# Attention outputs split as they come, a second bias buffer, the second norm inside its operands' loop, and small products ordered behind columns

## The chip, the cores and the metric

The kernel runs on one core of one Trainium2 chip. The metric is the device time of one execution in microseconds (us); three executions of the kernel before took 1672.16, 1673.4 and 1676.07 us. The core has TensorE (PE, matrix products into PSUM), VectorE (DVE), ScalarE (ACT), GpSimd (POOL) and SyncE (SP, which here mostly issues DMAs).

## The reference

Two requests of 512 tokens, 1024 wide, go through the same two layers: layer 0 is a bidirectional RWKV-7 time mixing, layer 1 a neighbourhood attention over an 8 x 64 grid of tokens. Each layer has a norm before it and one after it.

```python
def _trunk(x, pre_norm_g, post_norm_g, rwkv_params, na_params):
    for i in range(DEPTH):
        xn = _rms_norm(x, pre_norm_g[i])
        h = _rwkv7_branch(xn, ...) if i % N_MIXERS == 0 else _natten_branch(xn, ...)
        x = x + _rms_norm(h, post_norm_g[i])
    return x

def _natten_branch(xn, w_in, b_in, rpb, w_o, b_o):
    proj = xn @ w_in + b_in
    q, k, v, z = jnp.split(proj, 4, axis=-1)
    o = _neighbourhood_attention(heads(q) * (HEAD_DIM ** -0.5), heads(k), heads(v), rpb)
    return (o.reshape(bsz, t, D_INNER) * jax.nn.silu(z)) @ w_o + b_o
```

In `_neighbourhood_attention` each token attends to its 8 x 16 window with a learned bias per head, through a softmax.

## The kernel before, in words

Activations lie with channels on the 128 partitions and the 512 tokens along the free axis: a (1024 x 512) activation is eight tiles of 128 x 512. The requests are s = 0 and s = 1.

A weight product is made in *columns*: one column is 128 output channels, 8 steps over k, and 3 matmuls a step, because every float32 operand is split into a high part (a cast on ACT, L377) and a low part (a subtraction on DVE, L378), and hi·hi, hi·lo and lo·hi are summed (L428 to L430, one PSUM bank `pg`, two banks in all). A column is 24 matmuls. Its weights come by two DMAs into three `raw` buffers and are split the same way into `whi` and `wlo`.

The program has two parts. Up to some 1170 us the recurrent scan of layer 0 runs, in an order planned by hand. Then `rest` runs, and there the order is made by the tile scheduler: instructions are recorded by generators that `run` interleaves in given shares, and the scheduler places each one by its priority (the order of recording, moved by `high_priority`) when its inputs are ready in its own timeline. What it fixes is the order of the instructions on each engine; each engine then works its list in that order. `behind` adds an ordering edge between two instructions of one engine, without a wait.

The steps of `rest`, in the order of recording:

- `inproj(0, ...)`: the last two groups of columns q, k, v, z of request 0; `qkvz` takes a column out of `pg` by a product with the norm's `rstd` on DVE (L1398) and stores it to DRAM.
- `heads(s, p)`: attention for a pair of heads, in two half-heads of two column blocks. Loads of bias, q, k, v; scores on PE (`sc`, L1442, one buffer); on DVE score plus bias with its maximum (L1453); exponent on ACT (L1456); reciprocal and scaling on DVE (L1457, L1458); transposes on PE (`pt`, L1460); copies on ACT (`pts`, L1463); the product with v on PE (`po`, L1475; v is transposed by L1429). Last, `po` is multiplied by the gate z on DVE (L1484). For s = 0 the result is kept as float32 (`oa`) and split later.
- `out0(1)`: the output columns of layer 0 for request 1 into the tiles `h`, with their sum of squares (L1315, L1325, L1327).
- `out1(0)`: the output columns of attention for request 0. It first splits all eight `oa` (`operands`), into the `act` buffers, then makes the columns (L1499 takes them out of `pg`), then `rstd`, then two last operations a tile on DVE (L1506, L1507) and the store of the result.
- `norm0(1)`: post-norm, residual and next norm's sum for request 1: `rstds`, then for each of 8 tiles two operations on DVE (L1358, L1359), a square on ACT (L1360) and a sum on DVE (L1364); all of it at a raised priority, through `ahead`. Then `x1n(1)` splits the eight tiles for the next product (L1379 on ACT, L1380 on DVE), into `act` buffers that `out1(0)` must have left.
- `by_token`: 32 transposes of `h` (L1518) in eight groups of four into `pm` banks, copied by ACT (L1520) and stored, for the last product.
- `inproj(1, ...)` with `heads(1, p)`, and `last()`.

`rstds` (L449) turns a sum of squares into 1/sqrt on every partition: four matmuls against ones (L456), a root on ACT (L459), a reciprocal and four diagonal tiles on DVE (L461, L464), four matmuls that spread them (L468), a copy on ACT (L470).

Of the kernel before, what the change touches and what calls it, by code (L numbers as in the profile page):

```python
# [11 lines left out]
F32 = mybir.dt.float32  # L12
F32R = mybir.dt.float32r
AF = mybir.ActivationFunctionType
ALU = mybir.AluOpType
# [4 lines left out]
P = 128  # L20
T = 512
D = 1024
KT = D // P
NP = 8
# [207 lines left out]
class Trunk:  # L232
# [6 lines left out]
    LA = -40  # L239
    LATER = (0, 40, 0, 0)  # L240
    POST4 = 0.2
    LAST = ("pg", "pg", "po", "pm")
# [6 lines left out]
    NA = 1000  # L249
    SUMS, SG, ZY = 0, 0, 2  # L250
    CH, FIRST, WFIRST = 100, 17, 3
    NVS = 2
# [169 lines left out]
    def gemm(self, w, x, tag):  # L422

        nc = self.nc
        ps = self.p(tag)
        for k in range(KT):
            hi, lo = w[k]
            nc.tensor.matmul(ps, hi, x[k][0], start=(k == 0), stop=False)  # L428
            nc.tensor.matmul(ps, hi, x[k][1], start=False, stop=False)  # L429
            nc.tensor.matmul(ps, lo, x[k][0], start=False, stop=(k == KT - 1))  # L430
            if k < KT - 1:
                yield
        return ps
# [12 lines left out]
        run(self.rstds(acc))  # L446
        return acc

    def rstds(self, acc):  # L449

        nc = self.nc
        free, room = self.bank()
        yield "P", free, room
        ps = self.p("pm", (P, 4))
        for c in range(4):
            nc.tensor.matmul(ps[:, c:c + 1], acc[:, c * P:(c + 1) * P], self.ones[:, 0:1], start=True, stop=True)  # L456
        yield "A"
        r = self.t("rs", (P, 4), 2)
        nc.scalar.activation(r, ps, AF.Sqrt, bias=self.eps[:, 0:1], scale=1.0 / D)  # L459
        yield "D"  # L460
        nc.vector.reciprocal(r, r)  # L461
        dg = self.tmp()
        for c in range(4):
            nc.vector.tensor_scalar(dg[:, c * P:(c + 1) * P], self.ident, r[:, c:c + 1], None, op0=ALU.mult)  # L464
        yield "P", free, lambda c: max(room(c), c.at([dg.tensor.name]))
        out = self.p("pm")
        for c in range(4):
            nc.tensor.matmul(out[:, c * P:(c + 1) * P], self.ones, dg[:, c * P:(c + 1) * P], start=True, stop=True)  # L468
        yield "A"
        nc.scalar.copy(acc, out)  # L470

# [867 lines left out]
    def norm0(self, s):  # L1339

        nc = self.nc
        if s == 0:
            yield "P", lambda: ("h", s) in self.made
            self.x1_acc = self.t("vs", bufs=self.NVS)
            yield from self.rstds(self.h_acc)
            self.made.add(("hr", s))
            yield "P", lambda: self.did["x1s"] == KT, lambda c: c.at([self.x1_acc.tensor.name])
            yield from self.rstds(self.x1_acc)
            self.x1_rstd = self.x1_acc
            self.made.add(("x1", s))  # L1350
            return
        rstd = self.h_acc
        yield from self.rstds(rstd)
        acc = self.t("vs", bufs=self.NVS)
        for k in range(KT):
            h = self.h[k]
            x = self.load(self.t("xr", bufs=self.NXR), self.a["xc"][s][k * P:(k + 1) * P, :])
            nc.vector.scalar_tensor_tensor(h, h, self.vec("post0", k), rstd, op0=ALU.mult, op1=ALU.mult)  # L1358
            nc.vector.tensor_tensor(h, h, x, op=ALU.add)  # L1359
            nc.scalar.activation(x, h, AF.Square)  # L1360
            if k == 0:
                nc.scalar.activation(acc, h, AF.Square)
            else:
                self.adder(s, k + 1).tensor_tensor(acc, x, acc, op=ALU.add)  # L1364
            yield
        yield "P"
        yield from self.rstds(acc)
        self.x1_rstd = acc
        self.made.add(("x1", s))

    def adder(self, s, k):
        return self.nc.vector if s and k % 2 else self.nc.vector

    def x1n(self, s):

        out = []
        for k, h in enumerate(self.h):
            lo, hi = self.pair()
            self.nc.scalar.activation(hi, h, AF.Identity, scale=self.vec("pre1", k))  # L1379
            self.nc.vector.scalar_tensor_tensor(lo, h, self.vec("pre1", k), hi.bitcast(F32), op0=ALU.mult, op1=ALU.subtract)  # L1380
            out.append((hi, lo))
        return out


    def inproj(self, s, x, p, cs=range(4)):

# [6 lines left out]
    def qkvz(self, s, p, c, ps):  # L1393
        act, vt = self.nc.scalar, self.nc.vector
        kind = ("q1", "k1", "v1", "z1")[c]
        yield "D", lambda: ("x1", s) in self.made, lambda c, n=ps.tensor.name: c.at([n, self.x1_rstd.tensor.name])
        o = self.tmp()
        vt.tensor_tensor(o, ps, self.x1_rstd, op=ALU.mult)  # L1398
        ps = o
        yield "A"  # L1400
        if c == 0:
            act.activation(o, ps, AF.Identity, scale=0.125, bias=self.dv[:, 48 + p:49 + p])
        elif c == 1:
            act.activation(o, ps, AF.Identity, bias=self.vec("bin", 8 + p))
        elif c == 2:
            act.activation(o, ps, AF.Identity, scale=0.5, bias=self.dv[:, 64 + p:65 + p])
        else:
            th = self.tmp()
            act.activation(th, ps, AF.Tanh, scale=0.5, bias=self.dv[:, 56 + p:57 + p])
            act.activation(o, ps, AF.Identity, bias=self.vec("bin", 24 + p))  # L1410
            yield "D"
            vt.scalar_tensor_tensor(o, th, 1.0, o, op0=ALU.add, op1=ALU.mult)
        self.save(kind, s, p, o)

    def heads(self, s, p):

        nc = self.nc
        vt, act, gps = nc.vector, nc.scalar, nc.gpsimd
# [13 lines left out]
        op = self.p("po", (P, 4, P))  # L1432
        cols = (0, 8, 24, 32)
        for ns in ((0, 1), (2, 3)):
# [13 lines left out]
            for n in ns:  # L1448
                pt = self.p("pt", (P, 2, 2, P))
# [30 lines left out]
                            last = one  # L1480
            yield
        with self.tc.high_priority(self.HP[s] if p == NP - 1 else 0):
            o = self.tmp() if s else self.t("oa", (P, T), NP, F32, self.ap)
            vt.tensor_tensor(o, op.rearrange("p n t -> p (n t)"), z, op=ALU.mult)  # L1484
            if s:
                lo, hi = (self.t("os", (P, T), 2 * NP, F32R, self.ap) for _ in range(2))
                o = self.halves(o, lo, hi)
        self.os[s].append(o)
        yield

    def out1(self, s):
        nc = self.nc
        x = self.operands(lambda k: self.os[s][k])
        acc = self.t("acc1", pool=self.ap)
        hs = []
        for p in range(NP):
            ps = yield from self.gemm(self.weight(self.a["w_ao"][p]), x, self.OUT1[p % 4])
            h = self.t("os", (P, T), 2 * NP, F32R, self.ap).bitcast(F32)
            nc.scalar.activation(h, ps, AF.Identity, bias=self.vec("bo", p))  # L1499
            self.sumsq(acc, h, p, nc.vector if p == NP - 1 else nc.vector)  # L1500
            hs.append(h)
            yield
        rstd = self.rstd(acc)
        for k, h in enumerate(hs):
            x = self.load(self.t("xr", bufs=self.NXR), self.sp["x1", s, k])
            nc.vector.scalar_tensor_tensor(h, h, self.vec("post1", k), rstd, op0=ALU.mult, op1=ALU.mult)  # L1506
            (nc.vector if k % 2 else nc.vector).tensor_tensor(h, h, x, op=ALU.add)  # L1507
            nc.sync.dma_start(self.a["y"][s][k * P:(k + 1) * P, :], h)
            yield

    def by_token(self):

        nc = self.nc
        for m in range(4):
            for c in range(2):
                ps = self.p("pm", (P, 4, P))
                for j in range(4):
                    nc.tensor.transpose(ps[:, j], self.h[4 * c + j][:, m * P:(m + 1) * P], self.ident)  # L1518
                x = self.tmp()
                nc.scalar.copy(x, ps.rearrange("p j c -> p (j c)"))  # L1520
                self.save("xt", c, m, x)
                yield
# [229 lines left out]
    def rest(self, prep, mid):  # L1752
# [34 lines left out]
        while queue:  # L1787
            next(a)
        self.last()

    def ahead(self, g):

        while True:
            with self.tc.high_priority(self.NA):
                if next(g, self) is self:
                    return
            yield


class Step:  # L1800
# [122 lines left out]
```

## Time and profile before

| what | value |
|---|---|
| three runs, us | 1672.16, 1673.4 (median), 1676.07 |
| the profiled execution, us | 1673.62 |
| its span, first to last instruction, us | 1671.8 |
| time outside the span, us | 1.8 |
| mean granted TensorE clock | 0.974 |
| DVE, ACT busy | 74%, 59% of the span |

The profile is one execution. An engine's row in its timeline has the start (us from the span's start), the time taken, the instruction by line and tile, how many were merged, and in brackets the idle time of the engine before it with what ended that idle time. A table by stretches gives the busy time of each engine, the granted clock of TensorE (1.00 is full speed) and the load of the DMA engines.

### The profile page before, as it was taken

The page shows a single profiled execution, that of the slowest core. Times are in us where ns is not written, and L with a number is a line of the kernel's source. Part 1 is how long each engine was busy: PE and PEld are TensorE (multiplying, and loading weights), DVE is VectorE, ACT ScalarE, POOL GpSimd, SP SyncE. Part 2 cuts the span into 40 slices and gives each one's busy share as a digit, 9 for nine tenths or more (in the row PEclk, how much of TensorE's full clock was granted, in tenths as well). Part 3 has the DMA queues.
Part 4 walks back from the last instruction along what each step waited for, and adds up shares of the span by engine and source line. Part 5 has one row for each costly group of instructions (what it writes and reads, how often), then busy time and mean ns, then how long its engine had stood idle before and what let it go on. Part 6 is the DMA issues. An engine that isn't in the chain of part 4 may idle for free.

```text
span 1671.8 us, 46461 instructions
## 1 busy us (share of the span) xinstructions
PE 1566.5 (94%) x18834; PEld 1200.3 (72%) x18834; DVE 1229.4 (74%) x2725; ACT 982.8 (59%) x1977; POOL 116.9 (7%) x246
## 2 busy tenths in 40 slices
PE   7989897999999988999998999999999898999998
PEld 6867666776767766766776777777778687777776
DVE  8985667788877885897888897855676856554564
ACT  5443665766766667655675665454577655554562
POOL 0000102310101122000000000000000000000000
PEclk9989998999999997999998999999999999999999
DMA  6435678677687786776776665563774337545553
GB/s 210 164 126 187 200 259 270 199 240 225 214 258 239 220 268 184 232 249 198 239 235 217 204 225 189 169 193 128 269 239 150 116 114 263 178 158 176 160 175 107
DMA packets 204470, 336.27 MB, mean 201 GB/s; under 512 B 20928, under 2 KB 86592, under 8 KB 204256
## 3 DMA queue, kind: packets, MB, share of 16 engines
q1 hardware_dynamic: 194144, 301.84, 56.4%
q0 software_dynamic: 10112, 31.47, 5.7%
q8 instruction: 148, 2.42, 0.6%
q14 instruction: 66, 0.54, 0.1%
HBM read 227.71 MB, written 105.51 MB: 199 GB/s over the span
## 4 chain that ended last, share of the span: by engine, by line
PE 68%; DVE 12%; DMA 9%; ACT 7%; issue 4%; SPq 1%; DVEq 0%; ACTq 0%
PE pm L807 7%; PE pm L808 5%; PE pm L809 5%; PE pg L428 5%; PE pg L429 5%; PE pg L430 5%; PE pf L1095 3%; PE zy L1167 2%; PE us L1214 2%; PE sc L1442 2%; PE us L1194 2%; PE zy L1218 2%; PE po L1475 2%; PE pt L1460 2%; DMA dab<-ab 1%
## 5 line engine op out<-in xcount | busy, mean ns | idle before, releaser
L807 PE MATMUL pm<-act,whi 128*128 128x512 f32 x640 | 285.5, 446 | 12.7 <-ACT act L776 4.1
L808 PE MATMUL pm<-act,whi 128*128 128x512 f32 x640 | 256.5, 401 | 9.8 <-DVE act L754 5.9
L809 PE MATMUL pm<-act,wlo 128*128 128x512 f32 x640 | 255.7, 400 | 7.9 <-DVE wlo L728 7.8
L428 PE MATMUL pg<-act,whi 128*128 128x512 f32 x448 | 182.6, 409 | 6.1 <-ACT act L377 5.7
L429 PE MATMUL pg<-act,whi 128*128 128x512 f32 x448 | 178.0, 397 | 0.1
L430 PE MATMUL pg<-act,wlo 128*128 128x512 f32 x448 | 177.0, 395 | 0.0
L377 ACT CAST whi<-raw 128x512 fp32r<-128x512 f32 x148 | 91.5, 619 | 125.2 <-PE pg L429 80.7
L807 PEld LDWEIGHTS pm<-act,whi 128*128 128x128 f32 x640 | 122.0, 191 | 56.2 <-issue 11.6
L809 PEld LDWEIGHTS pm<-act,wlo 128*128 128x128 f32 x640 | 122.3, 191 | 38.9 <-DVE wlo L728 12.1
L378 DVE TENSOR_TENSOR wlo<-raw,whi 128x512 fp32r<-128x512 f32 x148 | 101.3, 687 | 66.0 <-ACT whi L377 58.8
L808 PEld LDWEIGHTS pm<-act,whi 128*128 128x128 f32 x640 | 122.8, 192 | 35.8 <-DVE act L754 11.1
L728 DVE TENSOR_TENSOR wlo<-raw,whi 128x512 fp32r<-128x512 f32 x160 | 108.9, 685 | 41.4 <-ACT whi L726 41.2
L726 ACT CAST whi<-raw 128x512 fp32r<-128x512 f32 x160 | 97.9, 618 | 55.4 <-PE pm L808 38.5
L428 PEld LDWEIGHTS pg<-act,whi 128*128 128x128 f32 x448 | 84.6, 189 | 24.8 <-ACT act L377 6.0
L430 PEld LDWEIGHTS pg<-act,wlo 128*128 128x128 f32 x448 | 84.8, 189 | 18.7 <-issue 1.2
L429 PEld LDWEIGHTS pg<-act,whi 128*128 128x128 f32 x448 | 84.9, 190 | 17.2 <-issue 1.7
L999 DVE TENSOR_TENSOR etmp<-N 128x30 f32<-128x30 f32 (+14 forms) x240 | 78.5, 327 | 4.1
L1001 DVE TENSOR_TENSOR N<-etmp,N 128x30 f32<-128x30 f32 (+14 forms) x240 | 78.5, 327 | 3.8
L1453 DVE CUSTOM_DVE_ANT_0 sb<-sc,bias 128x256 f32<-128x256 f32 x128 | 49.4, 419 | 28.9 <-PE pt L1460 22.9
L1456 ACT ACTIVATE sb<-sb,mx 128x256 f32<-128x256 f32 x128 | 64.0, 505 | 8.7 <-DVE mx L1455 8.6
L1206 ACT COPY X<-us 64x256 f32<-64x256 f32 x128 | 46.8, 366 | 35.6 <-PE zy L1073 32.9
L1095 PE MATMUL pf<-cab 64*64 64x128 f32 (+1 forms) x2048 | 66.3, 266 | 0.7 <-issue 0.7
(396 smaller groups left out, 3465.3 us busy)
## 6 DMA issues: line engine op xcount, KB each, us to landing
dab<-ab SPq DMA_DIRECT2D x32, 1024.0 KB
cab<-dab SPq DMA_DIRECT2D x64, 512.0 KB
raw<-in_w_in_dram SPq DMA_DIRECT2D x128, 256.0 KB
bias<-in_rpb_dram SPq DMA_DIRECT2D x32, 384.0 KB
raw<-in_w_z_dram SPq DMA_DIRECT2D x32, 256.0 KB
raw<-in_w_k_dram SPq DMA_DIRECT2D x32, 256.0 KB
raw<-in_w_r_dram SPq DMA_DIRECT2D x32, 256.0 KB
k<-dk SPq DMA_DIRECT2D x32, 256.0 KB
```

Of the source, the lines that this page charges most:

```text
L377: self.nc.scalar.copy(hi, src)
L378: (eng or self.nc.vector).tensor_tensor(lo, src, hi.bitcast(F32), op=ALU.subtract)
L428: nc.tensor.matmul(ps, hi, x[k][0], start=(k == 0), stop=False)
L429: nc.tensor.matmul(ps, hi, x[k][1], start=False, stop=False)
L430: nc.tensor.matmul(ps, lo, x[k][0], start=False, stop=(k == KT - 1))
L726: nc.scalar.copy(hi, raw[h])
L728: nc.vector.tensor_tensor(lo, raw.pop(h), hi.bitcast(F32), op=ALU.subtract)
L807: nc.tensor.matmul(ps, hi[:, at], xh, start=(k == 0), stop=False)
L808: nc.tensor.matmul(ps, hi[:, at], xl, start=False, stop=False)
L809: nc.tensor.matmul(ps, lo[:, at], xh, start=False, stop=(k == KT - 1))
L999: vt.tensor_tensor(tv, N[:, q + 1:, q:q + 1].broadcast_to([P, n, q]), N[:, q:q + 1, :q].broadcast_to([P, n, q]), op=ALU.mult)
L1095: end = nc.tensor.matmul(st.f[half(a), h, 0, d, g] if st.last else st.f[half(a), h, :, d, g], ab[half(h), d, g, 2 * e[d] + 1 - a], rt if s ...
```

## The change

- `heads(0, p)` splits its output as soon as it is there, into the `os` buffers (for s = 1 it did so before); `out1` takes those tiles as they are and puts its own results into `oa`. `operands` for `out1(0)` is gone, with its 8 casts and 8 subtractions in that place; the same 16 operations now stand in `heads`.
- The attention bias has two buffers (`NBI` 2 for 1), so that the bias of the next head pair can be loaded early.
- `norm0(1)` makes the split operands (`x1n` before) in its own loop, a tile at a time, and runs without raised priority, with up to three steps of `out1(0)` for each of its own.
- The matmuls of `rstds` in `norm0(1)` and in `out1(0)` are ordered behind the last column matmul recorded so far (`self.mm`); the transposes of `by_token` likewise, and they use `pt` banks.
- The first of the two last operations of `out1` is ordered behind the latest L1398 on DVE (`self.mq`).

```diff
-    NAB, NX, NR, NY, NSB, NBI = 2, 2, 2, 2, 4, 1
+    NAB, NX, NR, NY, NSB, NBI = 2, 2, 2, 2, 4, 2
...
-            nc.tensor.matmul(ps, lo, x[k][0], start=False, stop=(k == KT - 1))
+            self.mm = nc.tensor.matmul(ps, lo, x[k][0], start=False, stop=(k == KT - 1))
...
-    def rstds(self, acc):
+    def rstds(self, acc, mm=None):
...
+            if mm:
+                self.behind(one, mm())
...
-        yield from self.rstds(rstd)
+        yield from self.rstds(rstd, lambda: self.mm)
         acc = self.t("vs", bufs=self.NVS)
+        self.x1 = []
         for k in range(KT):
...
+            lo, hi = self.pair()
+            nc.scalar.activation(hi, h, AF.Identity, scale=self.vec("pre1", k))
+            nc.vector.scalar_tensor_tensor(lo, h, self.vec("pre1", k), hi.bitcast(F32), op0=ALU.mult, op1=ALU.subtract)
+            self.x1.append((hi, lo))
             yield
...
-            o = self.tmp() if s else self.t("oa", (P, T), NP, F32, self.ap)
+            o = self.tmp()
             vt.tensor_tensor(o, op.rearrange("p n t -> p (n t)"), z, op=ALU.mult)
-            if s:
-                lo, hi = (self.t("os", (P, T), 2 * NP, F32R, self.ap) for _ in range(2))
-                o = self.halves(o, lo, hi)
+            lo, hi = (self.t("os", (P, T), 2 * NP, F32R, self.ap) for _ in range(2))
+            o = self.halves(o, lo, hi)
...
-        x = self.operands(lambda k: self.os[s][k])
+        x = self.os[s]
...
-            h = self.t("os", (P, T), 2 * NP, F32R, self.ap).bitcast(F32)
+            h = self.t("oa", (P, T), NP, F32, self.ap)
...
-        rstd = self.rstd(acc)
+        yield from self.rstds(acc, lambda: self.mm)
+        rstd = acc
...
-            nc.vector.scalar_tensor_tensor(h, h, self.vec("post1", k), rstd, op0=ALU.mult, op1=ALU.mult)
+            one = nc.vector.scalar_tensor_tensor(h, h, self.vec("post1", k), rstd, op0=ALU.mult, op1=ALU.mult)
+            self.behind(one, self.mq)
...
-                ps = self.p("pm", (P, 4, P))
+                ps = self.p("pt" if self.TOK else "pm", (P, 4, P))
                 for j in range(4):
-                    nc.tensor.transpose(ps[:, j], self.h[4 * c + j][:, m * P:(m + 1) * P], self.ident)
+                    one = nc.tensor.transpose(ps[:, j], self.h[4 * c + j][:, m * P:(m + 1) * P], self.ident)
+                    self.behind(one, self.mm)
...
-        run(self.ahead(self.norm0(1)), (o, KT * NP / 17))
-        x = self.x1n(1)
+        n = KT * NP
+        for _ in self.norm0(1):
+            for _ in range(min(n, 3)):
+                next(o)
+                n -= 1
+        for _ in range(n):
+            next(o)
+        x = self.x1
```

Up to the first matmuls of attention the two programs have the same order on every engine, and again near the end, for the last 934 instructions of PE and the last 342 of DVE. Between them the order differs at three places that matter below. Lines are renumbered by the change: L1442, L1460, L1475, L1429, L1484 and L1398 of before are L1437, L1455, L1470, L1424, L1479 and L1393 of the changed kernel, L1358 is L1363, L1359 is L1364, L464 is L466, L468 is L470, L1518 is L1514. Numbers behind a name tell tiles apart.

First place: PE at the start of attention for request 0. Before, columns (`pg`) stand between the groups of the first head pair:

```order
L428 MATMUL pg_16990<-act_12319,whi_16986 128x512
L1429 MATMUL pm_16609<-cc,v_2897_16594 128x128 x2
L1442 MATMUL sc_16712<-k_2896_16592,q_2895_16590 128x256 x4
L1429 MATMUL pm_16609<-cc,v_2897_16594 128x128
L1460 MATMUL pt_16623<-cc,sb_16624 128x128 x2
L1460 MATMUL pt_16623<-cc,sb_16636 128x128 x2
L1460 MATMUL pt_16658<-cc,sb_16659 128x128 x2
L429 MATMUL pg_16990<-act_12318,whi_16986 128x512
L430 MATMUL pg_16990<-act_12319,wlo_16987 128x512
L428 MATMUL pg_16990<-act_12387,whi_16986 128x512
L1460 MATMUL pt_16658<-cc,sb_16684 128x128 x2
```

Now three half-heads stand there without a column (`sc_16712` is the second half of the first pair, `sc_16848` belongs to the second pair, whose bias has the second buffer):

```order
L430 MATMUL pg_16892<-act_12484,wlo_16889 128x512
L1424 MATMUL pm_16609<-cc,v_2897_16594 128x128 x3
L1437 MATMUL sc_16712<-k_2896_16592,q_2895_16590 128x256 x4
L1455 MATMUL pt_16623<-cc,sb_16624 128x128 x2
L1455 MATMUL pt_16623<-cc,sb_16636 128x128 x2
L1455 MATMUL pt_16658<-cc,sb_16659 128x128 x2
L1455 MATMUL pt_16658<-cc,sb_16684 128x128 x2
L1424 MATMUL pm_16830<-cc,v_2953_16821 128x128 x4
L1470 MATMUL po_16617<-pts_16699,vtok_16599 64x128 x4
L1470 MATMUL po_16617<-pts_16648,vtok_16599 64x128 x4
L1437 MATMUL sc_16848<-k_2952_16819,q_2951_16817 128x256 x4
L1424 MATMUL pm_16839<-cc,v_2953_16821 128x128 x3
```

The column that stood between them (`pg_16990` of before) comes 12 rows further down; on DVE the two L1398 that empty the banks of the columns before it have moved behind the softmax of the second pair.

Second place: DVE around the last head pair of request 0. Before, the product of that pair (L1484, `oa_18379`) stands behind eight L1358 of `norm0(1)` (the last four are shown; the other four, and the diagonals of L464, stand ahead of them) and four more operations:

```order
L1358 SCALAR_TENSOR_TENSOR hh_17976<-hh_17976,cv,acc_17537 128x512
L1358 SCALAR_TENSOR_TENSOR hh_18078<-hh_18078,cv,acc_17537 128x512
L1358 SCALAR_TENSOR_TENSOR hh_18196<-hh_18196,cv,acc_17537 128x512
L1358 SCALAR_TENSOR_TENSOR hh_18298<-hh_18298,cv,acc_17537 128x512
L1359 TENSOR_TENSOR h_3136_17538<-h_3136_17538,xr_18538 128x512
L378 TENSOR_TENSOR wlo_18523<-raw_18516,whi_18522 128x512
L1359 TENSOR_TENSOR h_3163_17638<-h_3163_17638,xr_18556 128x512
L1359 TENSOR_TENSOR h_3189_17756<-h_3189_17756,xr_18592 128x512
L1484 TENSOR_TENSOR oa_18379<-po_18249,z_3343_18369 128x512
```

Now the product and its low part (`os_18409`) stand ahead of them:

```order
L463 RECIPROCAL rs_18453<-rs_18453 128x4
L378 TENSOR_TENSOR wlo_18535<-raw_18528,whi_18534 128x512
L1479 TENSOR_TENSOR tmp_18407<-po_18277,z_3357_18397 128x512
L466 TENSOR_SCALAR tmp_18481<-cc,rs_18453 128x128 x4
L378 TENSOR_TENSOR os_18409<-tmp_18407,os_18410 128x512
L1363 SCALAR_TENSOR_TENSOR h_3142_17550<-h_3142_17550,cv,acc_17549 128x512
L1363 SCALAR_TENSOR_TENSOR h_3171_17654<-h_3171_17654,cv,acc_17549 128x512
```

What moved is the last head's product: from behind 12 operations to ahead of all of them.

Third place: PE where the two `rstds` of request 0's output and request 1's norm end, and `by_token` begins. Before, the products and five groups of transposes stand in one row, the first two groups being:

```order
L430 MATMUL pg_18989<-act_18923,wlo_18986 128x512
L468 MATMUL pm_18842<-tmp_18837,ones 128x128 x4
L468 MATMUL pm_18868<-tmp_18824,ones 128x128 x4
L1518 MATMUL pm_18954<-cc,h_3136_17538 128x128
L1518 MATMUL pm_18954<-cc,h_3163_17638 128x128
L1518 MATMUL pm_18954<-cc,h_3189_17756 128x128
L1518 MATMUL pm_18954<-cc,h_3217_17858 128x128
L1518 MATMUL pm_18996<-cc,hh_17976 128x128
L1518 MATMUL pm_18996<-cc,hh_18078 128x128
```

Now each group stands by itself among columns, and so do the products:

```order
L429 MATMUL pg_18879<-act_18629,whi_18875 128x512
L430 MATMUL pg_18879<-act_18630,wlo_18876 128x512
L1514 MATMUL pt_18895<-cc,h_3142_17550 128x128
L1514 MATMUL pt_18895<-cc,h_3171_17654 128x128
L1514 MATMUL pt_18895<-cc,h_3197_17772 128x128
L1514 MATMUL pt_18895<-cc,h_3227_17878 128x128
L428 MATMUL pg_18879<-act_18649,whi_18875 128x512
L429 MATMUL pg_18879<-act_18648,whi_18875 128x512
```

What moved are the columns: at least 15 of their matmuls stand between any two groups.

More of the change, by code (lines that the diff above doesn't have):

```diff
@@ L241 @@
     POST4 = 0.2
+    TOK = True
     LAST = ("pg", "pg", "po", "pm")
@@ L455, in rstds @@
         for c in range(4):
-            nc.tensor.matmul(ps[:, c:c + 1], acc[:, c * P:(c + 1) * P], self.ones[:, 0:1], start=True, stop=True)
+            one = nc.tensor.matmul(ps[:, c:c + 1], acc[:, c * P:(c + 1) * P], self.ones[:, 0:1], start=True, stop=True)
+            if mm:
+                self.behind(one, mm())
         yield "A"
@@ L467, in rstds @@
         for c in range(4):
-            nc.tensor.matmul(out[:, c * P:(c + 1) * P], self.ones, dg[:, c * P:(c + 1) * P], start=True, stop=True)
+            one = nc.tensor.matmul(out[:, c * P:(c + 1) * P], self.ones, dg[:, c * P:(c + 1) * P], start=True, stop=True)
+            if mm:
+                self.behind(one, mm())
         yield "A"
@@ L1363, in norm0 @@
             else:
-                self.adder(s, k + 1).tensor_tensor(acc, x, acc, op=ALU.add)
+                nc.vector.tensor_tensor(acc, x, acc, op=ALU.add)
+            lo, hi = self.pair()
+            nc.scalar.activation(hi, h, AF.Identity, scale=self.vec("pre1", k))
+            nc.vector.scalar_tensor_tensor(lo, h, self.vec("pre1", k), hi.bitcast(F32), op0=ALU.mult, op1=ALU.subtract)
+            self.x1.append((hi, lo))
             yield
         yield "P"
-        yield from self.rstds(acc)
+        yield from self.rstds(acc, lambda: self.mm)
         self.x1_rstd = acc
         self.made.add(("x1", s))
[L1371 to L1382, printed above, removed]
     def inproj(self, s, x, p, cs=range(4)):
@@ L1397, in qkvz @@
         o = self.tmp()
[L1398 removed]
+        self.mq = vt.tensor_tensor(o, ps, self.x1_rstd, op=ALU.mult)
         ps = o
@@ L1502, in out1 @@
             yield
-        rstd = self.rstd(acc)
+        yield from self.rstds(acc, lambda: self.mm)
+        rstd = acc
         for k, h in enumerate(hs):
             x = self.load(self.t("xr", bufs=self.NXR), self.sp["x1", s, k])
-            nc.vector.scalar_tensor_tensor(h, h, self.vec("post1", k), rstd, op0=ALU.mult, op1=ALU.mult)
+            one = nc.vector.scalar_tensor_tensor(h, h, self.vec("post1", k), rstd, op0=ALU.mult, op1=ALU.mult)
+            self.behind(one, self.mq)
             (nc.vector if k % 2 else nc.vector).tensor_tensor(h, h, x, op=ALU.add)
@@ L1789, in rest @@
         self.last()
[L1791 to L1797, printed above, removed]
 class Step:
```

1 line of the change is left out of this document (removed).

## The prediction

> **What bounds the kernel now.** I read the share of busy time first, then the busy time by stretches, then PE's timeline where a stretch is not full, and last the engine named as what ended the idle time.
>
> ```profile
> PE 1566.5 (94%) x18834; PEld 1200.3 (72%) x18834; DVE 1229.4 (74%) x2725; ACT 982.8 (59%) x1977; POOL 116.9 (7%) x246
> ```
>
> PE is busy 94% of the span, so the change, which takes no matmul away, can only win where PE stands still or runs at a low clock. From the table by stretches (stretch, then busy time of PE, PEld, DVE, ACT, POOL, granted clock, DMA share, GB/s), a full stretch and the two poor ones:
>
> ```profile
> 1225.00:1250.00 25.00, 25.00 (x172) 19.95 (x171) 19.77 (x75) 19.23 (x48) 0.00 (x0) 1.00 0.71 238
> 1328.00:1335.00 7.00, 5.88 (x12) 3.78 (x13) 6.49 (x11) 5.60 (x12) 0.00 (x0) 0.51 0.40 128
> 1380.00:1390.00 10.00, 5.85 (x36) 4.17 (x35) 8.81 (x14) 4.85 (x8) 0.00 (x0) 1.00 0.53 179
> ```
>
> In the full one PE is busy all 25.00 us: there the change can lose, and cannot win. The first poor one is the end of request 0's last head pair; its PE, DVE and ACT rows are:
>
> ```profile
> 1321.84 1.09 PE L1475 MATMUL po<-pts,vtok 128*64 128x128 f32 x16
> 1328.67 1.22 PE L428 MATMUL pg<-act,whi 128*128 128x512 f32 x2 [5.74 <-ACT act L377]
> ...
> 1335.04 0.40 PE L428 MATMUL pg<-act,whi 128*128 128x512 f32 x1
> 1335.28 0.39 PE L429 MATMUL pg<-act,whi 128*128 128x512 f32 x1
> ```
> ```profile
> 1319.57 2.74 DVE L1358 SCALAR_TENSOR_TENSOR h<-h,cv,acc 128x512 f32<-128x512 f32 x4 [1.74 <-ACT acc L470]
> 1322.23 2.73 DVE L1358 SCALAR_TENSOR_TENSOR hh<-hh,cv,acc 128x512 f32<-128x512 f32 x4
> ...
> 1327.29 0.68 DVE L1484 TENSOR_TENSOR oa<-po,z 128x512 f32<-128x512 f32 x1
> ```
> ```profile
> 1328.00 0.62 ACT L377 CAST act<-oa 128x512 fp32r<-128x512 f32 x1
> ```
>
> PE's last product with v could feed DVE's L1484 at about 1322.9 (5.74 before 1328.67). DVE comes to it only at 1327.29, since the eight L1358 that wait for nothing but the norm's `acc` stand ahead and run from 1319.57 to about 1325. Then ACT casts the tile and PE goes on. The matmuls that follow start at half clock: 0.51 in the stretch. From 1322.93 (1328.67 less 5.74) to 1335.04, when the pitch is again 1335.28 less 1335.04, 0.24 us, 12.1 us pass, in which 12 matmuls are made, 2.9 us of work at that pitch. The place costs 9.2 us: 5.7 of idle time and 3.5 that are nearly all low clock.
>
> [...]
>
> **The norm's operands and the last head.** The changed order puts the product (L1479) ahead of all eight L1363, then the four diagonals of `rstds` (L466), then the low part. PE's remaining wait is my estimate: the product (0.68) and the four diagonals, which the products of `rstds` behind it need, take
>
> ```profile
> 1316.95 0.88 DVE L464 TENSOR_SCALAR tmp<-cc,rs 128x128 f32<-128x128 f32 x4
> ```
>
> 0.68 and 0.88, so 1.55, and about 0.85 more, a copy by ACT and a cast (L377 took 0.62), until the first bank of the output columns is emptied. That is 2.4 us of idle time in two or three pieces, each below the 5.74 that went before half clock, and I take the clock to hold. **9.2 less 2.4: −6.8 us**. The ends are the little that rival B below leaves, and all 9.2. The same sixteen splits of the attention outputs are made as before, only earlier, in heads that have DVE time over.
>
> **The small products and the way back to tokens.** Now the second poor stretch: two products of `rstds` and five groups of transposes that stand in one row, both products, the first group and the last:
>
> ```profile
> 1379.11 1.05 PE L468 MATMUL pm<-tmp,ones 128*128 128x128 f32 x8
> 1380.84 1.16 PE L468 MATMUL pm<-tmp,ones 128*128 128x128 f32 x8 [0.68 <-ACT acc L470]
> 1382.67 0.66 PE L1518 MATMUL pm<-cc,h 128*128 128x128 f32 x4 [0.68 <-ACT vs L470]
> ...
> 1388.10 0.66 PE L1518 MATMUL pm<-cc,h 128*128 128x128 f32 x4 [0.72 <-ACT tmp L1520]
> 1388.67 0.50 PE L428 MATMUL pg<-act,whi 128*128 128x512 f32 x1
> ```
>
> Each needs the one bank that ACT has just copied out of the way, and PE waits for that every time. The row takes 1388.67 less 1379.11, 9.56 us. What four such 128x128 matmuls cost among columns is seen where v is transposed:
>
> ```profile
> 1297.56 0.39 PE L430 MATMUL pg<-act,wlo 128*128 128x512 f32 x1
> 1297.80 0.60 PE L1429 MATMUL pm<-cc,v 128*128 128x128 f32 x4
> 1298.15 0.48 PE L428 MATMUL pg<-act,whi 128*128 128x512 f32 x1
> 1298.46 0.40 PE L429 MATMUL pg<-act,whi 128*128 128x512 f32 x1
> ```
>
> From 1297.56 to 1298.46 are 0.90 us, in which two column matmuls take 0.45; the four take 0.45. In the changed order at least 15 column matmuls (3.5 us) stand between two groups, so that ACT's copy is done by then: five groups at 0.45 and two products of eight rows at 0.89 are 4.0 us. **9.56 less 4.0: −5.5 us.** What would undo it is an input that is late (the last tiles of the norm); DVE was busy 8.8 of 10.0 there, but the tiles come in the order of the transposes. The ends are 0 and these 5.5.
>
> **The start of attention.** With two bias buffers the softmax of the second pair is recorded and placed ahead of the evictions that free the `pg` banks, so three half-heads stand on PE without a column between. A half-head costs PE, by starts, and DVE, from its first L1453 to its last L1458:
>
> ```profile
> 1308.64 1.09 PE L1475 MATMUL po<-pts,vtok 128*64 128x128 f32 x16
> 1309.67 1.14 PE L1442 MATMUL sc<-k,q 64*128 64x256 f32 x8
> 1310.73 1.09 PE L1460 MATMUL pt<-cc,sb 128*128 128x128 f32 x8
> 1311.58 0.48 PE L428 MATMUL pg<-act,whi 128*128 128x512 f32 x1
> ```
> ```profile
> 1311.84 0.42 DVE L1453 CUSTOM_DVE_ANT_0 sb<-sc,bias 128x256 f32<-128x256 f32 x1
> ...
> 1315.36 0.35 DVE L1458 TENSOR_SCALAR sb<-sb,mx 128x256 f32<-128x256 f32 x1
> ```
>
> PE: 1.03 and 1.06 and 0.85, with 0.45 for four transposes of v, 3.4 us. DVE: 1315.71 less 1311.84, 3.9 us. If the scores of the next half are ready while DVE works, PE loses 3.9 less 3.4, 0.5 us, three times: **+1.4 us**. The ends: 0, and all of DVE's 3.9 exposed beside 0.45 of transposes, three times 3.4, or 10.3. I take the lower part, because the scores' buffer comes free after the four L1453, 1.4 us, and PE can fill it while ACT and DVE finish.
>
> **The second and third pair.** Some 40 to 60 us further on (the full stretch above), DVE's list has up to eight low parts of `out0(1)`'s operands between the softmaxes of two halves. One is 688 ns:
>
> ```profile
> L378 DVE TENSOR_TENSOR wlo<-raw,whi 128x512 fp32r<-128x512 f32 x116 | 79.6, 688 | 62.6 <-ACT whi L377 57.2 <-PE pg L429 2.0 <-PE pg L430 1.6
> ```
>
> Eight are 5.5 us. DVE was busy 19.8 of 25 there, so it has 5.2 to spare; but PE's columns at that place wait for those same operands. Between 0 and 5.5 I take the middle: **+2.7 us**.
>
> **Loads and last operations.** A column of k goes through DRAM into the next pair's scores, and there was one wait:
>
> ```profile
> 1501.10 0.42 SPq L327 DMA_DIRECT2D dq<-tmp  x1
> 1505.14 0.32 SPq L333 DMA_DIRECT2D q<-dq  x1
> ...
> 1514.16 0.33 SPq L333 DMA_DIRECT2D k<-dk  x1
> ```
> ```profile
> 1517.23 0.70 PE L1442 MATMUL sc<-k,q 64*128 64x256 f32 x2 [0.62 <-DMA k<-dk]
> ```
>
> A store takes 4.0 (1505.14 less 1501.10) and the load 3.1 (1517.23 less 1514.16); with L1398 and the addition of k's own bias, two operations on the shape of the low parts above, 0.7 each, 8.5 us lie between a column's end and its use. The loads of the attention bias now go out a pair earlier, on the same queue, ahead of some of these. The changed order leaves one to two columns (24 times 0.23, 5.5 each) for it: **+0.5 us**, between −0.6 and 3. The last operations of `out1(0)`, L1506 and L1507, go behind a column's eviction. They are sixteen operations of DVE on the same 128x512 shape as the low parts above, some 11 us at 688 ns, for which nobody but the result's store waits, and that store lies far from the end: 0. The evictions L1398 that they stood ahead of come no later for it: 0 as well.
>
> **The sum.** −6.8 −5.5 +1.4 +2.7 +0.5 is −7.7, against the profiled execution's 1673.6 (span 1671.8 and 1.8 around it; the median of the runs is 1673.4): **1665.9 us**.
>
> **Rivals.** *B, the gap moves on.* The product comes early, but the eight L1363 (5.3 us, 1319.57 to about 1324.9) now stand between it and the weights' low parts, and the output columns wait for those. For it: DVE works its list in order. Against it: a column has 5.5 us of matmuls ahead. It gives back 5.3 of the 6.8: 1671.2.
>
> *C, the softmax runs ahead of the columns, slower.* An eviction that stands behind a softmax operation waits for all that this waits for; before, one L1453 waited
>
> ```profile
> 1204.37 0.42 DVE L1453 CUSTOM_DVE_ANT_0 sb<-sc,bias 128x256 f32<-128x256 f32 x1 [3.72 <-PE pt L1460]
> ```
>
> 3.72 us for PE to read a softmax tile. If at the start of attention the banks stay full for that reason, PE has neither columns nor scores: all 10.3, then 5.5 at the second and third pair, and 3.5 of low clock as above, 19.3 against gains of 12.3: 1680.6. It decides from 15.6 us of losses (12.3 and the 3.3 below). Against it: DVE has its inputs there. [...]
>
> *D, the low clock comes back.* Several short waits in a row, at the start of attention and behind the last head, bring the low clock at both places: twice 3.5 on top, 1672.9. Against it: the stretch of 1380 to 1390 with 4.17 us of idle time in pieces of 0.7 kept 1.00. [...]
>
> **How the numbers follow.** 0.2%, 3.3 us, is about what a measurement of this kernel can tell from no change. The forecast (A) has 0.62, with its own range of 1661 (all costs at 0: 1673.6 less 12.3) to 1670; B 0.13; C 0.13; D 0.12. Faster than 1670.1: A, and a quarter of B and of D, 0.68. Slower than 1676.7: most of C and a little of B and D, 0.14. The same: 0.18. The range of 1661 to 1675 takes in A, B and D; left out are C and a gain above 12.3.
>
> **Signs.** Right: behind request 0's last product with v PE idles 3 us at most and the clock stays at 1.00; no transpose group (L1514) has 0.7 idle ahead of it; from 1187 to 1250 PE idles about 4 us in all; L1437 waits for k at most 1 us. Wrong: over 15 us idle from 1187 to 1250 (C), a wait for `wlo` at L430 or the eviction of `pg` after the last head (B), a clock of about 0.5 in either place (D), or a new wait in the middle, 1420 to 1600, where I have none.

## The result and the profile after

Thirteen runs of the changed kernel have a median of 1664.6 us (1658.7 to 1672.0), thirteen of the kernel before, beside them, 1675.2; the medians differ by 10.6 us. The ratio over all these runs is 0.9932, 95% interval 0.9915 to 0.9948, which is 11.4 us of 1675.2, between 8.7 and 14.2. The profiled execution took 1666.92 us with a span of 1665.2, 6.6 less than before's span. The forecast was 1665.9 and 7.7 us faster. That the forecast time lies so close to the median is partly luck: the profile that it starts from, 1673.6, was 1.6 us below the median of before, and the forecast gain is some 3 us short.

First the share of busy time, then the table by stretches (columns as in the prediction), at the places that the prediction names. PE's busy time before is shown there: 25.00 of 25.00 in 1225 to 1250, and 5.88 of 7 at a clock of 0.51 at the last head. The row of before for the first stretch below is:

```profile
1185.00:1200.00 15.00, 15.00 (x82) 11.75 (x81) 10.68 (x47) 10.13 (x27) 0.00 (x0) 1.00 0.85 308
```

The rows of the changed kernel:

```profile
PE 1558.9 (94%) x18834; PEld 1195.1 (72%) x18834; DVE 1225.8 (74%) x2725; ACT 985.3 (59%) x1977; POOL 116.9 (7%) x246
```
```profile
1185.00:1200.00 15.00, 14.36 (x111) 10.86 (x109) 10.74 (x57) 10.11 (x30) 0.00 (x0) 1.00 1.04 400
1225.00:1250.00 25.00, 22.43 (x141) 17.48 (x139) 19.13 (x70) 19.85 (x47) 0.00 (x0) 1.00 0.71 231
1326.00:1333.00 7.00, 5.06 (x37) 3.85 (x36) 4.45 (x10) 3.62 (x7) 0.00 (x0) 1.00 0.13 37
1375.00:1400.00 25.00, 25.00 (x136) 20.17 (x135) 12.84 (x38) 14.19 (x28) 0.00 (x0) 1.00 0.55 182
```

PE now loses 0.6 and 2.6 us where it lost nothing, 1.9 us at the last head with the clock at 1.00, and nothing at all around the transposes. PE's rows at the last head, with DVE's beside them:

```profile
1326.19 1.09 PE L1470 MATMUL po<-pts,vtok 128*64 128x128 f32 x16
1328.37 0.91 PE L470 MATMUL pm<-tmp,ones 128*128 128x128 f32 x6 [1.08 <-DVE tmp L466]
...
1331.75 0.50 PE L428 MATMUL pg<-os,whi 128*128 128x512 f32 x1 [0.86 <-ACT oa L1493]
```
```profile
1327.34 0.69 DVE L1479 TENSOR_TENSOR tmp<-po,z 128x512 f32<-128x512 f32 x1 [1.93 <-PE po L1470]
1327.94 0.87 DVE L466 TENSOR_SCALAR tmp<-cc,rs 128x128 f32<-128x128 f32 x4
1328.72 0.68 DVE L378 TENSOR_TENSOR os<-tmp,os 128x512 fp32r<-128x512 f32 x1
1330.62 2.74 DVE L1363 SCALAR_TENSOR_TENSOR h<-h,cv,acc 128x512 f32<-128x512 f32 x4 [1.21 <-ACT acc L474]
```

DVE takes the product 1.15 us after PE starts its last product with v (5.45 before), and the norm's L1363 come 3.3 us later. Two waits are left, one for the product and the four diagonals (1.08), one for the first bank of the output columns (0.86).

The runs show a larger gain than the two profiles, so I kept one measure that leaves out the scan, whose length scatters: from PE's first score product to the start of the last product with v of request 0 (A), and from there to the end of the span (B). A and B are of single profiled executions; each ratio is to runs of before made beside that kernel's. The products of the norm's `rstds` (L468, 0.9 us) lie in A where A is 135.0 (before, e6, e10) and in B in all other kernels, so the A that compares with these others is 134.1.

| kernel | A, us | B, us | ratio to before, 95% interval |
|---|---|---|---|
| before, three profiles | 135.0, 135.0, 135.0 | 350.0, 351.7, 352.3 | 1 |
| changed, two profiles | 138.7, 138.8 | 339.0, 339.0 | 0.9932 [0.9915, 0.9948]; 0.9915 [0.9899, 0.9931] |
| e1, early split alone | 142.2 | 346.3 | 1.0007 [0.9992, 1.0022] |
| e2, ordered products and transposes alone | 134.1 | 343.1 | 0.9915 [0.9896, 0.9933] |
| e3, changed, one bias buffer | 141.1 | 338.7 | 0.9961 [0.9944, 0.9978] |
| e5, ordered products of `rstds` alone | 134.1 | 346.1 | 0.9953 [0.9934, 0.9971] |
| e6, ordered transposes alone | 135.0 | 356.2 | 1.0022 [1.0004, 1.0041] |
| e9, changed, last operations free | 138.5 | 338.9 | 0.9942 [0.9919, 0.9964] |
| e10, changed, late split | 135.0 | 345.4 | 0.9969 [0.9954, 0.9984] |
| e11 and e12, e2 with two bias buffers | 134.1, 134.1 | 338.2, 337.4 | 0.9918 [0.9897, 0.9938]; 0.9912 [0.9883, 0.9941] |

### The profile page after: what moved, and what is told of

Read it like the earlier page. It is cut to its first block, busy times and chain, and to the rows that moved or that the text cites. A ratio compares the mean times of both kernels' runs of the same rounds, so it can differ in the third digit from the quotient of the medians.

```text
span 1665.2 us, 46432 instructions
## 1 busy us (share of the span) xinstructions
PE 1558.9 (94%) x18834; PEld 1195.1 (72%) x18834; DVE 1225.8 (74%) x2725; ACT 985.3 (59%) x1977; POOL 116.9 (7%) x246
## 4 chain that ended last, share of the span: by engine, by line
PE 68%; DVE 10%; DMA 10%; ACT 8%; issue 4%; SPq 0%; DVEq 0%; POOL 0%; ACTq 0%; POOLq 0%
PE pm L811 7%; PE pm L813 6%; PE pg L428 6%; PE pm L812 5%; PE pg L429 5%; PE pg L430 5%; PE pf L1099 3%; PE zy L1171 2%; PE us L1218 2%; PE us L1198 2%; PE sc L1437 2%; PE zy L1222 2%; PE po L1470 1%; PE pt L1455 1%; PE zy L428 1%
## 5 line engine op out<-in xcount | busy, mean ns | idle before, releaser
L428 PE MATMUL pg<-act,whi 128*128 128x512 f32 x384 | 158.2, 412 | 0.4 <-DVE tmp L1393 0.4
L429 PE MATMUL pg<-act,whi 128*128 128x512 f32 x384 | 152.2, 396 | 0.0
L430 PE MATMUL pg<-act,wlo 128*128 128x512 f32 x384 | 151.9, 396 | 0.0
L428 PEld LDWEIGHTS pg<-act,whi 128*128 128x128 f32 x384 | 72.2, 188 | 15.8 <-issue 3.3
L430 PEld LDWEIGHTS pg<-act,wlo 128*128 128x128 f32 x384 | 72.2, 188 | 15.5 <-issue 0.7
L429 PEld LDWEIGHTS pg<-act,whi 128*128 128x128 f32 x384 | 72.4, 189 | 13.1 <-issue 1.5
```

The source lines that it names most:

```text
L430: self.mm = nc.tensor.matmul(ps, lo, x[k][0], start=False, stop=(k == KT - 1))
```

## The experiments

**e1, the early split alone.** In the kernel before:

```diff
-            o = self.tmp() if s else self.t("oa", (P, T), NP, F32, self.ap)
+            o = self.tmp()
-            if s:
-                lo, hi = ...
-                o = self.halves(o, lo, hi)
+            lo, hi = ...
+            o = self.halves(o, lo, hi)
-        x = self.operands(lambda k: self.os[s][k])
+        x = self.os[s]
```

> The kernel before, with one part of the change: heads of request 0 split their output as it comes, and out1 takes those tiles. Theory (the early split is what closes the gap at the last head): behind the last product with v of request 0 PE idles about 2 us instead of 5.74, the granted clock there stays at 1.00 instead of 0.51 (7 us gained), the row of transposes still has its idle times of 0.7 (nothing gained there), and 1187 to 1250 us loses about 3 us, as in the changed kernel. Sum about -4 us, ratio 0.9975. Rival (the norm in its operands' loop, or its lost priority, is what closes the gap): the 5.74 us stay, ratio 1.000 or above.

It is level with before. PE at the start of attention, at the last head and at the row of transposes:

```profile
1201.68 1.99 PE L1442 MATMUL sc<-k,q 64*128 64x256 f32 x8 [2.44 <-DVE mx L1453]
...
1331.07 0.91 PE L468 MATMUL pm<-tmp,ones 128*128 128x128 f32 x6 [1.08 <-DVE tmp L464]
...
1385.17 0.66 PE L1517 MATMUL pm<-cc,hh 128*128 128x128 f32 x4 [0.68 <-ACT tmp L1519]
1386.56 1.12 PE L1517 MATMUL pm<-cc,h 128*128 128x128 f32 x4 [0.73 <-ACT tmp L1519]
```

The gap closes as the theory has it. But A is 7.1 us longer (8.0 against 134.1), not 3: the second pair waits for its softmax (2.44; e3 shows that the one bias buffer is in it), and the eight score matmuls behind that wait take 1.99 us where they took 1.13, with the granted clock at 0.66 from 1201 to 1206. The row of transposes slows too, in its middle (0.66 a group, then 1.12). So the loss at the start comes with the early split, here in a kernel with one bias buffer.

**e2, the ordered products and transposes alone.**

```diff
-        yield from self.rstds(rstd)
+        yield from self.rstds(rstd, lambda: self.mm)
...
-                ps = self.p("pm", (P, 4, P))
+                ps = self.p("pt", (P, 4, P))
...
+                    self.behind(one, self.mm)
```

> The kernel before, with one part of the change: the products of rstds and the transposes of by_token ordered behind columns, the transposes in pt banks. Theory: the seven idle times of 0.7 us between 1379 and 1389 go, 5.5 us in all, the last head's gap (5.74 us, clock 0.51) and the full stretch 1187 to 1250 stay; ratio 0.9967. Rival (the groups are bound by their inputs or by ACT's copies, so the idle time moves to another place): no change of the sum of PE's idle time, ratio 1.000.

Both the theory and the rival missed: the row is gone, as expected, but so is the gap at the last head, without an early split.

```profile
1323.61 0.73 PE L428 MATMUL pg<-act,whi 128*128 128x512 f32 x2 [1.44 <-ACT act L377]
...
1506.47 0.70 PE L1446 MATMUL sc<-k,q 64*128 64x256 f32 x2 [1.68 <-DMA k<-dk]
1507.10 1.17 PE L1479 MATMUL po<-pts,vtok 128*64 128x128 f32 x16
1508.19 2.07 PE L1446 MATMUL sc<-k,q 64*128 64x256 f32 x6
```
```profile
1322.22 0.69 DVE L1488 TENSOR_TENSOR oa<-po,z 128x512 f32<-128x512 f32 x1 [1.92 <-PE po L1479]
...
1328.86 2.73 DVE L1362 SCALAR_TENSOR_TENSOR h<-h,cv,acc 128x512 f32<-128x512 f32 x4
```

The product (L1488 here) starts as soon as PE is done, and the norm's eight operations (L1362) come at 1328.9, because the products of `rstds` that they wait for stand behind more columns (PE makes them at 1325.4, behind the last product with v; in the kernel before they stood ahead of it). The row had six idle times, 4.2 us, and not the seven of the expectation. Of the 5.74 us 1.44 are left. B is 343.1 and not less, mostly because of a stall of its own at 1506: a wait of 1.68 us for k, then six score matmuls in 2.07 us, and a granted clock of 0.60 from 1510 to 1516.

**e3, the changed kernel with one bias buffer** (`NBI` 1).

> The changed kernel with one bias buffer again (NBI 1); the order on PE, DVE, ACT and POOL is the same, that of the loads on SP differs. Prediction's cause for the loss at the start of attention (two bias buffers let the softmax run ahead of the columns): the idle times of PE between 1187 and 1250 (3.1 us) go, ratio to before about 0.991. Rival (they come from the early split): the 3.1 us stay or grow by waits for the bias, ratio 0.993 to 0.996.

The prediction's cause falls. PE's order has the same three half-heads without a column, and A grows from 138.7 to 141.1 with a wait in the middle of them:

```profile
1200.20 1.13 PE L1437 MATMUL sc<-k,q 64*128 64x256 f32 x8 [1.60 <-DVE mx L1448]
...
1237.95 1.13 PE L1437 MATMUL sc<-k,q 64*128 64x256 f32 x8 [1.60 <-DVE mx L1448]
```

DVE's rows show what the first one waits for:

```profile
1197.86 0.42 DVE L1448 CUSTOM_DVE_ANT_0 sb<-sc,bias 128x256 f32<-128x256 f32 x1 [1.58 <-DMA bias<-in_rpb_dram]
1198.81 0.42 DVE L1448 CUSTOM_DVE_ANT_0 sb<-sc,bias 128x256 f32<-128x256 f32 x1 [0.52 <-DMA bias<-in_rpb_dram]
```

This wait is not there with two buffers; the second, at 1237.95, is there with either. The second buffer takes away 2.4 us of what the early split costs; it does not cause the cost. Why the scheduler lets the softmax run ahead once the split stands in `heads`, no run shows.

**e4, the changed kernel again.**

> The changed kernel once more, unaltered. If the profile's difference is the whole effect (6.7 us): ratio 0.996. If the thirteen runs are right: 0.993. A second profile also shows how much of its time before 1130 us, where the two programs have the same order, varies from one execution to the next: a us or more, or less.

The ratio is 0.9915, and A and B are as in the first profile to 0.2 us. Up to the first score product this execution took 1186.1 us, the first 1187.5. So the changed kernel is steady from attention on in these two executions, and the difference between runs and profiles has to come from the kernel before or from the scan.

**e5 and e6, the two halves of e2.** e5 has only the edges in `rstds`, e6 only those in `by_token` and the `pt` banks.

> The kernel before with only the products of rstds ordered behind columns (in norm0(1) and out1(0)). Theory (this edge alone closes the last head's gap: with it the eight L1358 that wait for the norm's acc come behind the product with the gate): idle time there about 1.5 us with clock 1.00, the row of transposes stays in one piece, and its short idle times may bring the low clock; about -7 us, ratio 0.996. Rival (it was the transposes' order that moved the gap): 5.7 us stay, ratio 1.000.

> The kernel before with only the transposes of by_token ordered behind columns, in pt banks. Theory: the 5.74 us and the clock of 0.51 at the last head stay, the row of transposes is spread and its idle times of 0.7 go: 5 us in the profile, and more in the median if the row of before comes at half clock in most executions (8 us, ratio 0.995). Rival: the row's gain is already covered by the rstds edge, ratio 1.000.

e5 closes the gap (1.44 us left) and keeps the row. e6 is a little slower than before (the interval begins at 1.0004), which neither side expected. DVE and PE where the row stood:

```profile
1386.10 5.39 DVE L1506 SCALAR_TENSOR_TENSOR os<-os,cv,acc 128x512 f32<-128x512 f32 x8 [0.73 <-ACT acc L470]
1391.41 1.28 DVE L1507 TENSOR_TENSOR os<-os,xr 128x512 f32<-128x512 f32 x2
1392.62 1.28 DVE L1398 TENSOR_TENSOR tmp<-pg,vs 128x512 f32<-128x512 f32 x2
```
```profile
1393.35 0.80 PE L428 MATMUL pg<-act,whi 128*128 128x512 f32 x1 [6.07 <-DVE tmp L1398]
```

With the transposes spread, the columns come earlier, and their evictions L1398 stand behind the first of the two last operations of `out1` for all eight tiles (5.39 us) and the second for two (1.28). PE has no free bank and waits 6.07 us, and the matmuls behind it go slowly (0.80 the first, then a pitch of 0.43 up to 1396.5, against 0.23 from 1396.9 on). The gain of the row turns into a longer wait. In e2, where the products of `rstds` are ordered too, two of these evictions come ahead of the eight operations (1374.3 against 1376.4).

**e7 and e8, the kernel before, two more profiles.**

> The kernel before, unaltered, for a second profile. Theory (the medians differ by more than the first two profiles because the first profile of before is a lucky one: in most executions the row of short idle times at the transposes drops TensorE to half clock): L1518 groups of 1.1 us instead of 0.66 and the stretch from 1129 us to the end 3 to 4 us longer than 543. Rival (the difference lies elsewhere or is scatter): the row is as before, within 0.5 us.

> The kernel before, unaltered, a third profile, for the same question: does the row of transposes run at half clock (theory, 3 to 4 us more) or as in the first profile (rival)?

The row ends at a low clock in both: 0.50 from 1392 to 1396 in e7, 0.51 from 1387 to 1394 in e8. From e8:

```profile
1386.22 0.65 PE L1518 MATMUL pm<-cc,h 128*128 128x128 f32 x4 [0.73 <-ACT tmp L1520]
...
1389.38 1.11 PE L1518 MATMUL pm<-cc,h 128*128 128x128 f32 x4 [0.72 <-ACT tmp L1520]
1390.15 0.77 PE L428 MATMUL pg<-act,whi 128*128 128x512 f32 x1
1390.72 0.63 PE L429 MATMUL pg<-act,whi 128*128 128x512 f32 x1
```
```profile
1381.00:1387.00 6.00, 3.12 (x20) 2.22 (x20) 5.60 (x10) 2.44 (x5) 0.00 (x0) 1.00 0.35 122
1387.00:1394.00 7.00, 5.73 (x17) 4.56 (x18) 3.73 (x7) 2.42 (x4) 0.00 (x0) 0.51 0.90 280
```

Same idle times, same order as in the first profile, where every group took 0.66; here the last took 1.11, and the columns behind it run at a pitch of 0.42 to 0.57. B is 1.7 and 2.3 us longer than in the first profile, about half of the 3 to 4 that I expected. The profile on which the prediction was made was one of the better executions.

**e9, the changed kernel with the last operations of `out1` free.**

```diff
-            self.behind(one, self.mq)
```

> The changed kernel without the edge that puts the first of the two last operations of out1 (L1501) behind an eviction (L1393); then all eight L1501 and three of the second operations stand on DVE ahead of the next eviction. The prediction's step (these operations cost nothing wherever they stand): no new wait, ratio as the changed kernel, 0.992. Rival (DVE waits with them for out1's rstd and for xr, while both pg banks wait for their eviction): a wait of PE of about 6 us for L1393 and some us of low clock behind it, as seen with the transposes alone; ratio 0.996 to 0.998.

A and B are those of the changed kernel. PE is full where e6 stood still:

```profile
1382.00:1388.00 6.00, 6.00 (x33) 4.95 (x32) 1.98 (x3) 3.03 (x5) 0.00 (x0) 1.00 0.71 219
1388.00:1394.00 6.00, 6.00 (x37) 4.81 (x36) 4.22 (x15) 3.78 (x8) 0.00 (x0) 1.00 0.53 173
```

The eight operations run between two evictions here (L1393 at 1385.5 and at 1399.2), and PE does not wait for the second one, so this edge buys nothing. Its interval, 0.9919 to 0.9964, holds the changed kernel's 0.9932.

**e10, the changed kernel with the late split.**

> The changed kernel with the split of request 0's attention outputs put back to the start of out1. Theory (in the whole change it is the early split that closes the last head's gap, because its norm is recorded with out1's steps and the rstds edge then binds to an earlier column): the product with the gate again stands behind eight L1363 on DVE, the 5.7 us and the low clock return (9 us), the start of attention is full again (4 us gained); 4 to 6 us slower than the changed kernel, ratio 0.995 to 0.996. Rival (the rstds edge alone closes the gap here too): 4 us faster than the changed kernel, ratio 0.990.

As the theory had it. With the norm recorded between the steps of `out1`, the `rstds` edge binds to an earlier column: PE makes the products at 1321.2, ahead of the last product with v at 1323.6, where e5 makes them behind it, at 1327.7. The gap is back, longer than before:

```profile
1331.19 1.22 PE L428 MATMUL pg<-act,whi 128*128 128x512 f32 x2 [6.50 <-ACT act L377]
```

A is 3.6 us shorter than in the changed kernel and B 6.4 longer; with the 0.9 us of `rstds` counted in the same part, 4.5 and 7.3.

**e11 and e12, e2 with two bias buffers.** PE's order is that of e2.

> The kernel before with the ordered products and transposes and two bias buffers, nothing else; the order on PE as with one bias buffer, DVE's and ACT's but for two rows each. If the second bias buffer helps where the start of attention is full anyway: fewer waits for k after 1450 us (2.4 us with one buffer), ratio 0.990, faster than the changed kernel. If it does not: ratio 0.9915, as without it.

> The kernel before with the ordered products and transposes and two bias buffers once more, for a second profile and twice the runs: it has neither the loss at the start of attention nor the low clock at the last head. If it beats the changed kernel: ratio 0.989 to 0.991 and some 1183 us to the end 4 us shorter than there. If the two are level: 0.9915 to 0.993.

In both profiles PE waits for k at most 0.66 us at a time, and A plus B are 472.4 and 471.5, against 477.6 and 477.9 in the changed kernel. That is the least of all kernels here. The times do not tell the two apart: 0.9918 and 0.9912, with intervals about as wide as the difference would be. In the profiled executions the 5 to 6 us were nearly lost again before attention, where the first score product comes at 1190.9 and 1192.1, against 1187.5 and 1186.1; why, no run shows.

## Why the prediction was right, step by step

- **The last head, −6.8.** The size holds: 1.94 us of idle time are left where 2.4 were forecast, the clock stays at 1.00, so 9.2 less 1.9, 7.3. Two readings under it were off. Of the 3.5 us called nearly all low clock, the 12 matmuls at half clock (0.43 us apart) explain 2.3, and short waits for the low part and for a bank the other 1.2. And that each piece lay below 5.74 was no reason for the clock to hold: in e2 a wait of 1.68 us had 0.60 behind it (1510 to 1516). The step that puts it down to the early split holds for this kernel (e10) and for the split alone (e1). It is not the only way: the ordered products of `rstds` alone do the same in the kernel before (e5), since then the norm's operations are not ready when the product is.
- **The small products and transposes, −5.5.** No group has idle time ahead of it any more (PE 25.00 of 25.00 in 1375 to 1400). So the row of before gave up its 5.5. What the term missed is that this row costs some 2 us more in two of three profiles, where the granted clock at its end was 0.50 and 0.51.
- **The start of attention, +1.4, and the second and third pair, +2.7.** A grew by 3.6 us, and by 4.5 against 134.1, where the sum was 4.1: idle times of 0.29 twice at the start, then 1.57, 0.48 and 0.42 at the second stretch, and 1.5 in rows that count as busy, as in eight transposes at 1196.9 that took 1.46 for 1.09; how much of this belongs to which place I can't say. So the sum of the two terms holds in size. The cause given for the first was wrong. It is the early split, not the second bias buffer, with which the softmax runs ahead: with two buffers and no early split A is 135.0 (e10) and 134.1 (e11, e12). The buffer saves 2.4 of what the split costs (e3).
- **Loads and last operations, +0.5 and 0.** The waits for k are 0.59, 0.30 and 0.63, 0.9 more than before. The reason given, bias loads that go out earlier on the same queue, is not shown: with the second buffer the waits fall from 2.4 us in e2 to 1.0 and 0.7 in e11 and e12, and rise from 1.1 in e3 to 1.5 and 1.8 in the changed kernel. Where the 0.9 come from stays open. The last operations cost nothing with the edge or without (e9). But such operations can: 6.07 us in e6, where the evictions behind them come late, though I had said that nobody waits.
- **The sum.** In the first pair of profiles A and B fell by 7.4 us together, 7.7 forecast. B fell by 11.9 with the 0.9 us of `rstds` that moved into it set aside, and the terms that lie in it add to 11.8.
- **The rivals.** B did not come: no wait for `wlo` or for the eviction behind the last head beyond the 0.86. C came as far as its first step (4.5 us of loss in A, far from its 15.6) and was outweighed. With its low clock it showed in e1 (0.66 from 1201 to 1206), where the 8.0 us lost in A took back the whole gain. D was right about the kernel before and wrong about the changed one: the row of short waits ended at the low clock in two of three profiles (0.50 in e7, 0.51 in e8), and the change takes these waits away. The clock of 1.00 in 1380 to 1390, which I set against D, was that of one execution.
- **What is open.** Over three profiles of before and the two of the changed kernel, A and B together differ by 8.6 us. The medians differ by 10.6, and the ratio gives 11.4, interval 8.7 to 14.2. The other 2 to 3 us I can't place. The time up to the first score product scattered from 1186.1 to 1192.1 us over the profiles of all these kernels, which have the same order on PE, DVE and ACT there but for the last 3 us, with no pattern that I can see. The norm's new place was not tried by itself; e10, which differs from e11 in it and in the edge of the last operations, has 8.1 us more in A and B together.

## What to carry to other kernels

Where an engine works a list in order, an early finish can be bought in two ways: make the needed operation earlier, or make the unneeded ones in front of it later; the second was free here (e5, A 134.1), the first cost 4.5 us elsewhere. Short waits in a row can be worth more than their sum: behind those of the kernel before the granted clock was 0.50 and 0.51 in two of three profiles, and B 1.7 and 2.3 us longer than in the third. One profile at full clock doesn't show that they are harmless, so take a second. And an edge that helps alone may need another one beside it: the ordered transposes alone made the kernel a little slower (1.0022), with the ordered products it was 0.9915.

## What the chip showed that I had not expected

The low clock came without a long wait too. Behind a single one of 1.68 us (e2, up to 1506.5) six score matmuls took 2.07 us from 1508.2 on, the granted clock of 1510 to 1516 was 0.60, and the column matmuls went from a pitch of 0.43 us back to 0.23 at 1514.9. Behind one of 2.44 (e1, up to 1201.7) the clock of 1201 to 1206 was 0.66. Behind others the speed held: two of 1.60 in e3, after each of which eight score matmuls took 1.13 us; one of 1.57 in the changed kernel, with 1.00 from 1225 to 1250; one of 1.44 in e2, where the columns were at a pitch of 0.24 at 1324.7; one of 1.08 in the changed kernel, with 1.00 from 1326 to 1333.

Of the rows of six waits of 0.7 that of the first profile of before stayed at 1.00 and those of e7 (0.50 from 1392 on) and e8 (0.51 from 1387 on) did not, nor did that of e1, by the times of its groups (0.66, then 1.12). The first profile, to be laid beside the two stretches of e8 above:

```profile
1380.00:1386.00 6.00, 3.24 (x22) 2.22 (x20) 5.60 (x9) 2.34 (x4) 0.00 (x0) 1.00 0.37 127
1386.00:1393.00 7.00, 5.61 (x28) 4.43 (x28) 3.91 (x7) 3.13 (x5) 0.00 (x0) 1.00 0.89 272
```

PE idles 2.76 us of the first six here and 2.88 in e8, at 1.00 in both; in the next seven the clock is 1.00 here and 0.51 there. So an identical order ran at either clock. What decides, no run shows.
